# A tuned two-block network kernel on one core: elementwise tensor arithmetic taken off GpSimd and given to VectorE

## The chip, the core and the metric

The kernel runs on one NeuronCore of one Trainium2 chip. The core has five engines with an instruction queue each, which start their instructions in order: PE (TensorE, matrix products; PEld is its load of weights), DVE (VectorE), ACT (ScalarE), POOL (GpSimd) and SP (SyncE, which here only issues DMAs). The engines meet through semaphores. The metric is the device time of one execution in microseconds; lower is better.

## What is computed

A stream of 512 tokens by 1024 features goes through two blocks, all in float32. In outline:

```
first block, twice (l = 0, 1):
  h += rms_norm( mixer(rms_norm(h)) )         # dilated attention | short conv | gated delta rule, 4 heads
  h += rms_norm( cross_attention(rms_norm(h), rms_norm(mem)) )
  h += rms_norm( (silu(g) * u) @ w_down )     # g, u = split(rms_norm(h) @ w_gate_up), hidden width 2816
second block:
  x += gate * even_mixer(modulated rms_norm(x), ctx)   # two grouped attentions, rope, gates
  x += gate * odd_mixer(modulated rms_norm(x), ctx)    # 31-tap depthwise conv over tokens | 8 heads of local attention
  out = rms_norm(x)
```

Every `rms_norm` divides by the root of the mean square over the 1024 features plus 1e-6 and multiplies by a gain.

## The kernel before

The stream lies transposed: features on the 128 partitions, in 8 chunks, 512 tokens along the free axis (`hT`, 8 x 128 x 512). A matrix product keeps float32 accuracy in three passes: weights and inputs are each split in a high part and a low part of fewer bits (`wh` + `wl`, `xh` + `xl`), and `mm3` (L288 to L290) adds wh·xh, wh·xl and wl·xh in PSUM. `weight` loads a tile of 128 x 1024 weights (`wr`), ACT rounds it to `wh` (L258), DVE subtracts for `wl` (L262). So each of some 420 tiles of weights costs DVE one subtraction, and PE can't finish the tile's products before it is done.

The work of a chain (a softmax, a residual, a delta-rule step) is interleaved with independent products: `fill` holds generators, and `pump` takes a step of one between two steps of the chain. The kernel is recorded in that order; a scheduler then sets the order within each engine by when operands should be ready, so that the queues are not simply the order of the text. Which engine an elementwise operation runs on is written in the code: a number of tables (`SV`, `CSV`, `PSV`, `RPL`, `GV`, `CD`, `FIN`) say for single steps whether DVE or GpSimd does them.

The places that matter below:

- `residual`: for each of 8 chunks DVE makes `rt` = om · post · R (L397), then `hT += rt` (L398), on GpSimd for chunks 1, 3, 5, 7; ACT and DVE split the new chunk (L377, L378); PE multiplies it. `sumsq` squares a chunk on ACT and adds it to `acc`, mostly on GpSimd (L368); a product with ones sums over partitions (L355).
- `gdn_pair`: two heads of the gated delta rule. A chain of 30 short DVE instructions eliminates 16 columns (L982, L983), two more write `TT` (L985), PE transposes it (L993), GpSimd masks `AT` into `W` (L999). Meanwhile the fill projects the next heads: evacuation, convolution of 4 taps and `silu` (L440 to L444), whose last product is on GpSimd.
- `ffn`: per 128 hidden columns, DVE takes the gate product out of PSUM times R (`fg`, L427), `silu` follows, DVE takes the linear half out of PSUM times R (`fu`, L427), GpSimd multiplies the two (L1178). R is 1/rms of the norm before it.
- the odd mixer: 32 items of attention (softmax L707 to L725, transposes L735), and between them the 31 taps of `conv31` for 4 chunks. Chunks 0 to 2 use one fused DVE instruction per tap (L1715); chunk 3 multiplies on ACT (L1718) and adds on GpSimd (L1719). GpSimd also adds the column mask to the bias (L1642) and makes one of two low parts of each key (L695, beside DVE's L693).
- the end: `final` normalizes in two halves of 256 tokens, some pieces on GpSimd (L1218).

Of the kernel before, what the change touches and what calls it, by code (L numbers as in the profile page):

```python
# [29 lines left out]
SV = (2, 4, 6, 7)  # L30
CSV = (1, 3, 5, 7)
TS, TB = 2, 2
WP, XP = 1, 2
CD = 3
# [14 lines left out]
PSV = (1, 3, 5, 7)  # L49
LOH = 1  # L50
FIN = ((1, 0, 2), (1, 2, 4), (0, 4, 6), (0, 6, 8)), ((1, 0, 2), (1, 2, 4), (1, 4, 6), (0, 6, 7), (1, 7, 8))
Y1, Y2, Y3 = 2, 1, 2
GV = (1, 2, 3)
RPL = (1, 3, 5, 7)

# ------------------------------------------------------------------ small parameters, one column block each
# [14 lines left out]
def _consts():  # L71
    """Tables that depend on shapes alone."""
# [50 lines left out]
def _host(inp):  # L123
    """Lays the inputs out: transposes, tiles of the weights, rows and columns in the order of their use."""
# [22 lines left out]
    # second block  # L147
# [60 lines left out]
class Net:  # L208
    def __init__(self, ctx, tc, a, out):
# [21 lines left out]
        nc.vector.memset(self.epst[:, 2:3], EPS * 256.0)  # L231
        self.mod = [b.tile([128, 24, 2], F32, name=f"mod{i}") for i in range(2)]
# [15 lines left out]
    # ---- tiles of the weights, split in two parts of 12 bits  # L248
# [43 lines left out]
    def gemm_g(self, ap, x, done, n=512, k=KC, tag="g"):  # L292
        """done([128 columns of w]^T x, in PSUM), in pieces"""
# [22 lines left out]
    # ---- products that follow the chunks of their input as they are made  # L316
# [18 lines left out]
    # ---- work that is put between the steps of a chain  # L335
# [15 lines left out]
    # ---- 1/sqrt of (scale * sum over partitions + bias), on all partitions  # L351
    def rsqrt_of(self, ss, out, scale, epscol, n=512, lhs=None):
        nc = self.nc
        ps = self.bps()[:, :n]
        nc.tensor.matmul(ps, self.ones if lhs is None else lhs, ss, start=True, stop=True)  # L355
        nc.scalar.activation(out, ps, AF.Ln, bias=self.epst[:, epscol:epscol + 1], scale=scale)
        nc.scalar.activation(out, out, AF.Exp, scale=-0.5)

    def sumsq(self, acc, src, first, eng=None, t=None):
# [20 lines left out]
    # ---- residual: hT += norm(om) * post; the next norm's statistics in R and its input, without 1/rms, in xh + xl  # L380
    def residual_stat(self, c, ps, acc):
        nc = self.nc
        nc.scalar.copy(self.om[:, c], ps)
        self.sumsq(acc, ps, c == 0, nc.vector if c == KC - 1 else None)

    def residual(self, acc, post, pre=None, R=None, scale=1.0 / D, epscol=0, chunk=2):
# [3 lines left out]
        with self.hp(HA):  # L390
            self.rsqrt_of(acc, Rp, 1.0 / D, 0)
# [11 lines left out]
        if pre is not None:  # L403
            self.prestat(R, scale, epscol, PSV)

    def prestat(self, R, scale=1.0 / D, epscol=0, dve=()):
        nc = self.nc
        acc = self.tmp("acc2", bufs=1)
        for c in range(KC):
            self.sumsq(acc, self.hT[:, c], c == 0, nc.vector if c in dve else None)  # L410
        self.rsqrt_of(acc, R, scale, epscol)

    def start(self, tiles):
# [10 lines left out]
        self.prestat(self.R, dve=SV)  # L424
# [12 lines left out]
    def silu(self, out, x, t, mul=None):  # L437
        """out = x * sigmoid(x), x in SBUF"""
# [5 lines left out]
        (mul or nc.vector).tensor_mul(out, x, t)  # L444

    # ---- tables of the partial rotary embedding
# [30 lines left out]
    # ---- first block  # L477
    def first(self, dbg=None):
# [5 lines left out]
        for l in range(2):  # L484
# [5 lines left out]
            if l == 0:  # L490
                with tc.tile_pool(name="md", bufs=1) as p:
# [7 lines left out]
                    self.residual(acc, "f_post0", "mix_pre1", self.R, chunk=1)  # L499
                    self.drain()  # L500
                if dbg and dbg(self, f"h3_{l}"): return
            else:
# [6 lines left out]
                with tc.tile_pool(name="ctx", bufs=1) as p:  # L509
                    self.fill = [self.ctx_stream(p)]  # L510
                    acc = self.xo_ffn(l, dbg, 1)
                    self.residual(acc, "f_post1", chunk=1)
# [10 lines left out]
    def xo_ffn(self, l, dbg, chunk):  # L523
# [4 lines left out]
        self.residual(acc, f"x_post{l}", f"f_pre{l}", self.R, chunk=chunk)  # L528
# [44 lines left out]
    def mix_out(self, l):  # L573
        """the first half of the mixer's outputs as input of its last product"""
# [8 lines left out]
    def shortconv(self, l, c, w, x, p):  # L583
# [7 lines left out]
        nc.gpsimd.tensor_mul(cp[:, 2:514], t, u)  # L591
# [6 lines left out]
        nc.gpsimd.tensor_mul(self.om[:, 2 + c], o, b)  # L598

    def dilated_in(self, l, w, x, p):  # L600
# [3 lines left out]
        with self.tc.tile_pool(name=f"dx{l}", bufs=1) as q:  # L604
# [4 lines left out]
            def rotate(xs, g):  # L609
                for c in range(2):  # L610
                    d = qk[:, 2 * g + c]
                    nc.gpsimd.tensor_mul(xs[:, c], xs[:, c], CS[:, 1])
# [49 lines left out]
    def to_tok(self, v, out, n):  # L662
        """v [128 features, n*128 tokens] -> out [128 tokens, n, 128 features]"""
# [6 lines left out]
    def qstack(self, q, p, scale, n=512, bufs=2):  # L670
        """the two heads of a chunk: their high and low parts over 128 partitions"""
# [11 lines left out]
    def kstack(self, k, p, bufs=2, out=None, n=512, off=0):  # L683
# [4 lines left out]
        for e in range(2):  # L688
# [38 lines left out]
    def ptrans(self, P, out, idx):  # L727
        """128-key blocks of P [128 queries, keys] -> out [128 keys, block, 128 queries], block i to idx[i]"""
# [16 lines left out]
    # ---- gated delta rule, four heads  # L745
# [54 lines left out]
    def gdn_norm(self, l, O, i, p):  # L800
        """norm over the width of each head, times the gate, for 128 tokens"""
# [16 lines left out]
    def gdn_gate(self, l, h, w, x):  # L818
        o = self.om[:, 4 + h]
        yield from self.gemm_g(w[24 + h], x, lambda ps: self.evacR(o, ps))  # L820
        self.silu(o, o, self.tmp("rt"), self.nc.gpsimd)

    def gdn_rows(self, l, x, p, cols, rh, rl):
# [11 lines left out]
        # beta  # L835
# [3 lines left out]
        # -exp(a_log) * softplus(a + dt_bias)  # L839
# [12 lines left out]
        # exp(decay) and exp(decay at the chunk's end - decay)  # L852
# [4 lines left out]
        # cols: [token, pair, quantity, head]  # L857
# [4 lines left out]
        # beta * exp(decay)  # L862
# [8 lines left out]
    def gdn_in(self, l, h, w, x, p, f):  # L871
        """q, k, v of a head: projection, causal convolution, silu, norm of q and k"""
# [900 lines left out]
```

## Time and profile before

| | |
|---|---|
| time, median of 3 runs | 2667.45 us (2666.31 to 2668.95) |
| span of the profiled execution, first to last instruction | 2663.9 us, 3.5 us under the median |
| busy | PE 2493.7 (94%), DVE 1799.1 (68%), ACT 1374.8 (52%), POOL 562.6 (21%) |
| mean granted TensorE clock | 0.977 of full speed |

The profile does not give a device time for its own execution; the 3.5 us between its span and the median are taken as what lies around the span. Busy time counts a stretch once even if two instructions overlap. PE's busy time contains matmuls that wait in its pipeline, so 94% is no measure of how near it is to its peak.

### The profile page before, as it was taken

Reading aid. Unit: us, or ns where it says so; the run is one execution under the profiler, and the core shown is the slowest. Engines: PE = TensorE matmul, PEld = TensorE weight load, DVE = VectorE, ACT = ScalarE, POOL = GpSimd, SP = SyncE. Lnnn points to the kernel's source line nnn. Section 1 sums busy time; section 2 is a strip of 40 time slices with the busy share of each in tenths; the row PEclk is TensorE's granted clock in tenths of the full one; section 3 lists DMA queues with packets and bytes.
Section 4 is the critical chain, followed back from the end, with each engine's and each line's share of the span. In section 5 each row is a group of like instructions: output and inputs, shape, how many; then the busy total and the mean of one; then the engine's idle time right before and its main releaser. Section 6 shows DMA issues by size and latency. Waiting matters only on the chain. (4 is left out here: it accounts for less than half of the span.)

```text
span 2663.9 us, 35466 instructions
## 1 busy us (share of the span) xinstructions
PE 2493.7 (94%) x13052; PEld 2020.3 (76%) x13052; DVE 1799.1 (68%) x3064; ACT 1374.8 (52%) x2629; POOL 562.6 (21%) x437
## 2 busy tenths in 40 slices
PE   8999999899999999899998999999979999898898
PEld 6677788667888666777887778788867888686786
DVE  7985665389554578765756656665587666589964
ACT  6653554443433456434545544445356766447674
POOL 2343120120100323422102100002032012115432
PEclk9999999999999999999999999999989999899999
DMA  5132132456333433212412233234232012221111
GB/s 170 51 78 65 58 129 99 127 180 211 108 107 91 143 98 78 54 54 87 136 62 96 79 96 111 83 100 138 86 122 89 25 40 66 79 79 46 50 60 64
DMA packets 82781, 246.02 MB, mean 92 GB/s; under 512 B 13736, under 2 KB 25128, under 8 KB 81456
## 3 DMA queue, kind: packets, MB, share of 16 engines
q1 hardware_dynamic: 79344, 240.41, 28.8%
q0 software_dynamic: 704, 2.17, 0.5%
q10 hardware_dynamic: 2560, 1.18, 0.3%
q8 instruction: 103, 1.69, 0.3%
q14 instruction: 70, 0.57, 0.1%
HBM read 237.68 MB, written 2.89 MB: 90 GB/s over the span
## 5 line engine op out<-in xcount | busy, mean ns | idle before, releaser
L288 PE MATMUL g<-xh,wh 128*128 128x512 f32 (+1 forms) x1960 | 781.2, 400 | 28.7 <-ACT wh L258 9.0
L289 PE MATMUL g<-xl,wh 128*128 128x512 f32 (+1 forms) x1960 | 781.2, 399 | 8.5 <-DVE xl L378 4.8
L290 PE MATMUL g<-xh,wl 128*128 128x512 f32 (+1 forms) x1960 | 777.2, 397 | 0.0
L258 ACT CAST wh<-wr 128x1024 fp32r<-128x1024 f32 (+4 forms) x422 | 396.9, 944 | 551.5 <-PE g L289 415.8
L262 DVE TENSOR_TENSOR wl<-wr,wh 128x1024 fp32r<-128x1024 f32 (+4 forms) x422 | 494.5, 1175 | 178.8 <-ACT wh L258 176.7
L288 PEld LDWEIGHTS g<-xh,wh 128*128 128x128 f32 x1960 | 371.9, 190 | 116.1 <-ACT xh L377 9.0
L289 PEld LDWEIGHTS g<-xl,wh 128*128 128x128 f32 x1960 | 374.4, 191 | 89.7 <-DVE xl L378 9.2
L290 PEld LDWEIGHTS g<-xh,wl 128*128 128x128 f32 x1960 | 373.7, 191 | 79.2 <-issue 4.8
L1178 POOL TENSOR_TENSOR fu<-fu,fg 128x512 f32<-128x512 f32 x44 | 68.1, 1548 | 615.9 <-ACT wh L258 342.5
L368 POOL TENSOR_TENSOR acc<-acc,sq 128x512 f32<-128x512 f32 x68 | 102.6, 1509 | 403.6 <-ACT sq L367 378.5
L288 PE MATMUL g<-yh,wh 128*128 128x512 f32 x352 | 140.2, 399 | 6.8 <-DVE om L1161 2.7
L290 PE MATMUL g<-yh,wl 128*128 128x512 f32 x352 | 139.1, 396 | 2.1 <-DVE wl L262 2.1
L289 PE MATMUL g<-yl,wh 128*128 128x512 f32 x352 | 138.7, 395 | 0.0
L735 PE MATMUL b<-ident,P 128*128 128x128 f32 x608 | 93.8, 280 | 32.8 <-DVE P L725 15.1
L735 PEld LDWEIGHTS b<-ident,P 128*128 128x128 f32 x608 | 69.1, 142 | 61.4 <-issue 35.3
L741 ACT COPY pt<-b 128x512 f32<-128x512 f32 (+3 forms) x224 | 92.1, 451 | 43.9 <-PE b L735 42.8
L1161 DVE TENSOR_TENSOR om<-om,g 128x512 f32<-128x512 f32 x80 | 54.8, 685 | 64.1 <-PE g L290 63.6
L290 PE MATMUL s<-ch,wl 128*128 128x256 f32 x288 | 83.6, 290 | 10.2 <-DVE wl L262 10.2
L441 ACT ACTIVATE rt<-rt 128x512 f32<-128x512 f32 x76 | 48.1, 632 | 81.8 <-DVE rt L440 81.4
L719 ACT ACTIVATE P<-P,st 128x512 f32<-128x512 f32 (+4 forms) x96 | 66.1, 689 | 37.9 <-DVE st L713 24.4
L1382 PE MATMUL b<-pt,V 128*64 128x128 f32 x672 | 85.2, 275 | 0.0
L288 PE MATMUL s<-ch,wh 128*128 128x256 f32 x288 | 84.9, 295 | 0.0
(432 smaller groups left out, 4774.4 us busy)
## 6 DMA issues: line engine op xcount, KB each, us to landing
wr<-in_w_gu_dram SPq DMA_DIRECT2D x88, 512.0 KB, 3.3
wr<-in_w_in_dram SPq DMA_DIRECT2D x56, 512.0 KB, 3.3
wr<-in_ev_in_dram SPq DMA_DIRECT2D x40, 512.0 KB, 3.2
wr<-in_od_in_dram SPq DMA_DIRECT2D x36, 512.0 KB, 3.5
wr<-in_w_xkv_dram SPq DMA_DIRECT2D x32, 512.0 KB, 3.2
mw<-in_mod_w_dram SPq DMA_DIRECT2D x24, 512.0 KB, 3.5
mw<-in_mod_t_dram SPq DMA_DIRECT2D x24, 512.0 KB, 3.4
wr<-in_w_down_dram SPq DMA_DIRECT2D x56, 192.0 KB, 2.4
```

The lines of the kernel that those rows point to most:

```text
L258: nc.scalar.copy(hi[:, :k], raw[:, :k])
L262: nc.vector.tensor_sub(lo[:, c:e], raw[:, c:e], hi[:, c:e].bitcast(F32))
L288: mm(ps, wh, xh, start=first, stop=False)
L289: mm(ps, wh, xl, start=False, stop=False)
L290: mm(ps, wl, xh, start=False, stop=last)
L368: (eng or nc.gpsimd).tensor_add(acc, acc, t)
L719: nc.scalar.activation(P[:, c], src[i], AF.Exp, bias=one(2), accum_out=one(3 + i))
L735: nc.tensor.transpose(ps[:, 128 * i:128 * i + 128], P[:, 128 * (j + i):128 * (j + i) + 128], self.ident)
L741: nc.scalar.copy(out[:, idx[j + i]:idx[j + i] + e - i], ps[:, 128 * i:128 * e].rearrange("p (a b) -> p a b", b=128))
L1161: nc.vector.tensor_add(self.om[:, c], self.om[:, c], ps)
L1178: nc.gpsimd.tensor_mul(u, u, g)
L1382: nc.tensor.matmul(o[s], v, PT[e][:, k], start=j == 0, stop=j == len(blocks) - 1)
```

## The change

Every elementwise tensor instruction on GpSimd goes to DVE; only its memsets and DMAs stay. The tables that chose an engine vanish. Two places change their arithmetic. In `ffn` the linear half is no longer multiplied by R: DVE multiplies the PSUM tile by `fg` directly, and one multiplication per tile is gone. The output is then larger by 1/R per token, which the norm behind the feed-forward divides out, except for its epsilon; so the norm's sum of squares starts from epsilon over R squared (`zacc`, one ACT instruction from the sums that R itself comes from) and takes no other epsilon. In `conv31` chunk 3 uses the fused taps too.

```
     def sumsq(self, acc, src, first, t=None):
...
             nc.scalar.activation(t, src, AF.Square)
-            (eng or nc.gpsimd).tensor_add(acc, acc, t)
+            nc.vector.tensor_add(acc, acc, t)
...
                 nc.vector.scalar_tensor_tensor(t, self.om[:, c], self.sm(post, c), Rp, ALU.mult, ALU.mult)
-                (nc.gpsimd if c in RPL else nc.vector).tensor_add(self.hT[:, c], self.hT[:, c], t)
+                nc.vector.tensor_add(self.hT[:, c], self.hT[:, c], t)
...
+        ps = self.rsqrt_of(acc, R, scale, epscol)
+        if keep:
+            self.zacc = self.tmp("acc", bufs=1)
+            nc.scalar.activation(self.zacc, ps, AF.Identity, bias=self.epst[:, 3:4], scale=8.0 * EPS / D)
...
-        (mul or nc.vector).tensor_mul(out, x, t)
+        nc.vector.tensor_mul(out, x, t)
...
-            nc.gpsimd.tensor_sub(lo[o, c], k[s], h[s, c].bitcast(F32))
+            nc.vector.tensor_sub(lo[o, c], k[s], h[s, c].bitcast(F32))
...
-                nc.gpsimd.tensor_mul(P3(M[e]), P3(AT[:, e]), bc(lev[:, lvl]))
+                nc.vector.tensor_mul(P3(M[e]), P3(AT[:, e]), bc(lev[:, lvl]))
...
-                    self.evacR(u, self.gemm(a["w_gu"][l][2 * j + 1], x))
-                    nc.gpsimd.tensor_mul(u, u, g)
+                    nc.vector.tensor_mul(u, self.gemm(a["w_gu"][l][2 * j + 1], x), g)
...
-            if c < CD:
-                nc.vector.scalar_tensor_tensor(o[:, lo:hi], src, dw(k), o[:, lo:hi], ALU.mult, ALU.add)
-            else:
-                s = self.tmp("sq")[:, lo:hi]
-                nc.scalar.activation(s, src, AF.Copy, scale=dw(k))
-                nc.gpsimd.tensor_add(o[:, lo:hi], o[:, lo:hi], s)
+            nc.vector.scalar_tensor_tensor(o[:, lo:hi], src, dw(k), o[:, lo:hi], ALU.mult, ALU.add)
```

The same exchange of engine is made in `prestat`, `colstat`, `gate`, `rope2`, `shortconv`, `rotate`, the rest of `gdn_pair`, `mem_kv`, `conv_norm`, the bias of the odd mixer and `final`.

In numbers of instructions: GpSimd's queue goes from 442 to 61, DVE's from 3066 to 3406, ACT's from 2399 to 2370; PE's and SP's have as many as before. The scheduler sets the orders anew; three places on DVE's queue follow.

The end of the elimination of the first pair of heads in layer 0 (`c` and `pr` are the columns being eliminated, `wl` and `wr` weights, `W` the masked matrix, `TT` what PE transposes next). Before:

```order
L262 TENSOR_TENSOR wl_2012<-wr_2009,wh_2011 128x1024
L983 TENSOR_TENSOR c_164_1288<-c_164_1288,pr_1289 128x8x3
L982 TENSOR_TENSOR pr_1289<-W_1107,c_164_1288 128x8x2
L983 TENSOR_TENSOR c_164_1288<-c_164_1288,pr_1289 128x8x2
L982 TENSOR_TENSOR pr_1289<-W_1107,c_164_1288 128x8
L983 TENSOR_TENSOR c_164_1288<-c_164_1288,pr_1289 128x8
L985 TENSOR_TENSOR TT_1108<-c_164_1288,d_214 128x512 x2
L427 TENSOR_TENSOR om<-g_1777,R 128x512
```

And now:

```order
L984 TENSOR_TENSOR c_164_1289<-c_164_1289,pr_1290 128x8x2
L257 TENSOR_TENSOR wl_1860<-wr_1857,wh_1859 128x1024
L983 TENSOR_TENSOR pr_1290<-W_1108,c_164_1289 128x8
L257 TENSOR_TENSOR wl_1924<-wr_1921,wh_1923 128x1024
L984 TENSOR_TENSOR c_164_1289<-c_164_1289,pr_1290 128x8
L1000 TENSOR_TENSOR W_1108<-AT_1107,lev_213 128x512
L986 TENSOR_TENSOR TT_1109<-c_164_1289,d_215 128x512 x2
L1000 TENSOR_TENSOR W_1108<-AT_1107,lev_213 128x512
L445 TENSOR_TENSOR cvv_1640<-cvv_1640,rt_1645 128x512
```

The masks into `W` and the products of `silu` (L445) now stand in DVE's queue around `TT`.

The residual after the second feed-forward (`acc` with the number 17xx sums the squares for the next norm). Before:

```order
L397 SCALAR_TENSOR_TENSOR rt_16234<-om,small,R 128x512
L397 SCALAR_TENSOR_TENSOR rt_16250<-om,small,R 128x512
L398 TENSOR_TENSOR hT<-hT,rt_16234 128x512
L262 TENSOR_TENSOR wl_16302<-wr_16299,wh_16301 128x1024
L397 SCALAR_TENSOR_TENSOR rt_16253<-om,small,R 128x512
```

And now:

```order
L394 SCALAR_TENSOR_TENSOR rt_16197<-om,small,R 128x512
L394 SCALAR_TENSOR_TENSOR rt_16213<-om,small,R 128x512
L395 TENSOR_TENSOR hT<-hT,rt_16197 128x512
L395 TENSOR_TENSOR hT<-hT,rt_16213 128x512
L394 SCALAR_TENSOR_TENSOR rt_16216<-om,small,R 128x512
```

Both additions to `hT` of a pair of chunks are DVE's now, one behind the other.

The odd mixer, between two items of attention (`cu`, `ckv` and `R` hold the inputs of the conv's chunks, `K` the keys' low parts, `P` and `st` belong to the softmax). Before:

```order
L1715 SCALAR_TENSOR_TENSOR om<-ckv,small,om 128x510
L724 RECIPROCAL st_20321<-st_20321 128x1
L693 TENSOR_TENSOR K_2314_20204<-rt_20213,K_2313_20203 64x512
L725 TENSOR_SCALAR P_20320<-P_20320,st_20321 128x768
L713 TENSOR_SCALAR st_20396<-st_20396 128x1
L1715 SCALAR_TENSOR_TENSOR om<-ckv,small,om 128x511 x2
L1715 SCALAR_TENSOR_TENSOR om<-R,small,om 128x511
```

And now:

```order
L726 TENSOR_SCALAR P_20226<-P_20226,st_20227 128x768
L708 TENSOR_REDUCE st_20270<-s_20249 128x1
L694 TENSOR_TENSOR K_2310_20157<-rt_20168,K_2309_20156 64x512
L714 TENSOR_SCALAR st_20270<-st_20270 128x1
L696 TENSOR_TENSOR K_2310_20157<-rt_20168,K_2309_20156 64x512
L694 TENSOR_TENSOR K_2312_20159<-rt_20168,K_2311_20158 64x512
L696 TENSOR_TENSOR K_2312_20159<-rt_20168,K_2311_20158 64x512
```

Four low parts of keys stand there where DVE had two, and the taps of `cu` stand among those of the other chunks.

## Rows read from the trace of the kernel before

**Rows 1.** The page: busy time, share of the span, instructions of each engine.

```profile
PE 2493.7 (94%) x13052; PEld 2020.3 (76%) x13052; DVE 1799.1 (68%) x3064; ACT 1374.8 (52%) x2629; POOL 562.6 (21%) x437
```

**Rows 2.** Four stretches: us; busy (instructions) of PE, PEld, DVE, ACT, POOL; granted clock.

```profile
140.00:180.00 40.00, 33.81 (x146) 26.70 (x145) 38.65 (x71) 21.84 (x33) 13.02 (x13) 0.91 0.33 89
...
666.00:732.60 66.60, 66.60 (x294) 54.76 (x293) 39.34 (x49) 27.32 (x37) 9.84 (x6) 1.00 0.35 108
...
1928.00:1985.00 57.00, 38.79 (x211) 31.63 (x210) 50.03 (x61) 32.19 (x57) 21.38 (x13) 0.79 0.38 123
...
2399.00:2532.00 133.00, 111.33 (x648) 90.76 (x648) 131.12 (x225) 89.52 (x202) 68.42 (x46) 0.95 0.16 51
```

**Rows 3.** PE's waits: line, what it waited for, total us, times, longest.

```profile
PE b L993 <- DVE TT L985: 20.1, 6, 6.1
...
PE b L355 <- DVE acc L368: 12.5, 6, 3.6
...
PE s L290 <- DVE wl L262: 11.2, 3, 7.7
...
PE g L288 <- ACT xh L377: 6.8, 6, 2.9
```

**Rows 4.** Single lines: instructions, their ns min/median/max, first and last start.

```profile
L398 POOL TENSOR_TENSOR hT<-hT,rt x24: 1262/1680/2714, 353.6 to 1970.7; 128x512 f32<-128x512 f32 x24
L398 DVE TENSOR_TENSOR hT<-hT,rt x24: 674/682/1791, 354.9 to 1970.5; 128x512 f32<-128x512 f32 x24
```

**Rows 5.** Timeline, DVE and POOL, around 151 us: start, us, instruction.

```profile
150.96 1.37 DVE L982 TENSOR_TENSOR pr<-W,c 128x104 f32<-128x104 f32 x1
152.92 0.25 DVE L983 TENSOR_TENSOR c<-c,pr 128x104 f32<-128x104 f32 x1
...
150.89 1.32 POOL L444 TENSOR_TENSOR cvv<-cvv,rt 128x512 f32<-128x512 f32 x1 [2.38 <-ACT rt L443]
```

**Rows 6.** Timeline, DVE and POOL, at the end of that elimination.

```profile
173.30 3.32 DVE L985 TENSOR_TENSOR TT<-c,d 128x512 f32<-128x512 f32 x2
...
173.14 2.93 POOL L999 TENSOR_TENSOR W<-AT,lev 128x512 f32<-128x512 f32 x2 [1.98 <-DMA wr<-in_w_in_dram]
```

**Rows 7.** Groups on DVE and POOL, 2399 to 2532 us: count, busy us, mean ns.

```profile
L1715 DVE SCALAR_TENSOR_TENSOR om<-ckv,small,om 128x507 f32<-128x507 f32 (+14 forms) x41 | 37.2, 927 | 0.0
L725 DVE TENSOR_SCALAR P<-P,st 128x768 f32<-128x768 f32 x21 | 21.3, 1012 | 0.1
L1715 DVE SCALAR_TENSOR_TENSOR om<-R,small,om 128x511 f32<-128x511 f32 (+14 forms) x15 | 15.3, 1023 | 0.0
L262 DVE TENSOR_TENSOR wl<-wr,wh 128x1024 fp32r<-128x1024 f32 x11 | 15.2, 1380 | 0.0
...
L693 DVE TENSOR_TENSOR K<-rt,K 64x512 fp32r<-64x512 f32 x6 | 9.1, 1520 | 0.1
L723 DVE TENSOR_TENSOR st<-st 128x1 f32<-128x1 f32 x20 | 8.6, 432 | 0.1
...
L1719 POOL TENSOR_TENSOR om<-om,sq 128x500 f32<-128x500 f32 (+14 forms) x27 | 40.5, 1499 | 28.7 <-ACT sq L1718 28.0
L1642 POOL TENSOR_TENSOR rpb<-rpb,colm 128x896 f32<-128x896 f32 x4 | 9.1, 2264 | 2.2 <-DMA rpb<-in_rpb_dram 2.2
```

**Rows 8.** Timeline, DVE, with POOL idle from 2502.6 to 2505.1 us.

```profile
2502.65 1.20 DVE L262 TENSOR_TENSOR wl<-wr,wh 128x1024 fp32r<-128x1024 f32 x1
2503.77 0.61 DVE L725 TENSOR_SCALAR P<-P,st 128x768 f32<-128x768 f32 x1
2504.30 0.73 DVE L1715 SCALAR_TENSOR_TENSOR om<-R,small,om 128x499 f32<-128x499 f32 x1
2504.95 0.15 DVE L723 TENSOR_TENSOR st<-st 128x1 f32<-128x1 f32 x1
```

**Rows 9.** The page: the feed-forward's product on POOL; the last column is idle before.

```profile
L1178 POOL TENSOR_TENSOR fu<-fu,fg 128x512 f32<-128x512 f32 x44 | 68.1, 1548 | 615.9 <-ACT wh L258 342.5
```

**Rows 10.** Timeline, DVE, the last norm's second half.

```profile
2653.85 1.48 DVE L368 TENSOR_TENSOR acc<-acc,sq 128x256 f32<-128x256 f32 x1
```

More of the change, by code (lines that the diff above doesn't have):

```diff
@@ L355, in rsqrt_of, with sumsq @@
         nc.tensor.matmul(ps, self.ones if lhs is None else lhs, ss, start=True, stop=True)
-        nc.scalar.activation(out, ps, AF.Ln, bias=self.epst[:, epscol:epscol + 1], scale=scale)
+        bias = 0.0 if epscol is None else self.epst[:, epscol:epscol + 1]
+        nc.scalar.activation(out, ps, AF.Ln, bias=bias, scale=scale)
         nc.scalar.activation(out, out, AF.Exp, scale=-0.5)
-    def sumsq(self, acc, src, first, eng=None, t=None):
+        return ps
+    def sumsq(self, acc, src, first, t=None):
         nc = self.nc
@@ L383, in residual_stat, with residual @@
         nc.scalar.copy(self.om[:, c], ps)
-        self.sumsq(acc, ps, c == 0, nc.vector if c == KC - 1 else None)
-    def residual(self, acc, post, pre=None, R=None, scale=1.0 / D, epscol=0, chunk=2):
+        self.sumsq(acc, ps, c == 0)
+    def residual(self, acc, post, pre=None, R=None, scale=1.0 / D, epscol=0, chunk=2, aeps=0, keep=False):
         nc = self.nc
@@ L390, in residual @@
         with self.hp(HA):
-            self.rsqrt_of(acc, Rp, 1.0 / D, 0)
+            self.rsqrt_of(acc, Rp, 1.0 / D, aeps)
         self.pump(3)
@@ L435, in out_proj, with silu @@
         return acc
-    def silu(self, out, x, t, mul=None):
+    def silu(self, out, x, t):
         nc = self.nc
@@ L498, in first @@
                     self.begin([w[1][c] for c in range(TB)], XT[5])
-                    self.residual(acc, "f_post0", "mix_pre1", self.R, chunk=1)
+                    self.residual(acc, "f_post0", "mix_pre1", self.R, chunk=1, aeps=None)
                     self.drain()
@@ L511, in first @@
                     acc = self.xo_ffn(l, dbg, 1)
-                    self.residual(acc, "f_post1", chunk=1)
+                    self.residual(acc, "f_post1", chunk=1, aeps=None)
                     if dbg and dbg(self, f"h3_{l}"): return
@@ L527, in xo_ffn @@
         self.begin([w[c] for c in range(TB)], XT[1 + l])
-        self.residual(acc, f"x_post{l}", f"f_pre{l}", self.R, chunk=chunk)
+        self.residual(acc, f"x_post{l}", f"f_pre{l}", self.R, chunk=chunk, keep=True)
         if dbg: dbg(self, f"h2_{l}")
@@ L889, in gdn_in @@
             t = self.tmp("rt")
-            self.silu(o, o, t, nc.gpsimd)
+            self.silu(o, o, t)
             if n != "v":
@@ L1140, in ffn @@
         x = (self.xh, self.xl)
-        acc = self.tmp("acc", bufs=1)
+        acc = self.zacc
         n = 0
@@ L1162, in down @@
                     if hi == HC:
-                        self.sumsq(acc, self.om[:, c], c == 0, nc.vector if c == KC - 1 else None)
+                        self.sumsq(acc, self.om[:, c], False)
                 step()
@@ L1306, in colstat @@
         for c in range(KC):
-            self.sumsq(acc, src[:, c], c == 0, self.nc.vector if c in CSV else None)
+            self.sumsq(acc, src[:, c], c == 0)
         R = self.tmp("Rp", bufs=1)[:, :n] if R is None else R
@@ L1351, in gate @@
         t = self.tmp("sq")[:, :n]
-        self.silu(t, g, t, eng)
-        eng.tensor_mul(o, o, t)
+        self.silu(t, g, t)
+        nc.vector.tensor_mul(o, o, t)
     def attend(self, sp, Q, K, i, e, pieces):
@@ L1509, in gate @@
         def gate(m, j):
-            yield from self.gemm_g(a["ev_in"][10 * m + 6 + j], x, lambda ps: self.gate(ps, self.om[:, 4 * m + j], S, nc.vector if m and j in GV else None))
+            yield from self.gemm_g(a["ev_in"][10 * m + 6 + j], x, lambda ps: self.gate(ps, self.om[:, 4 * m + j], S))
         self.fill = [kv(0), q(0, 0)]
@@ L1619, in gate @@
         def gate(j):
-            yield from self.gemm_g(w[24 + j], x, lambda ps: self.gate(ps, self.om[:, 4 + j], S, nc.vector if j in GV else None))
+            yield from self.gemm_g(w[24 + j], x, lambda ps: self.gate(ps, self.om[:, 4 + j], S))
         self.fill = [qkv(0)]
@@ L1704, in conv31 @@
         yield
-        if c < CD:
-            nc.vector.tensor_scalar(o, u, dw(15), self.sm("dwb", c), ALU.mult, ALU.add)
-        else:
-            nc.scalar.activation(o, u, AF.Identity, bias=self.sm("dwb", c), scale=dw(15))
+        nc.vector.tensor_scalar(o, u, dw(15), self.sm("dwb", c), ALU.mult, ALU.add)
         for k in range(31):
@@ L1746, in conv_norm @@
             t = self.tmp("sq")
-            self.silu(o, o, t, nc.gpsimd)
+            self.silu(o, o, t)
             yield from self.gemm_g(w[8 + c], x, lambda ps: self.gate(ps, o, S))
```

63 lines of the change are left out of this document (27 added, 36 removed).

## The prediction

> **What bounds the kernel now.** I read the page first. PE is busy 2493.7 of the 2663.9 us [rows 1], so at most 170.2 us is idle on PE, and the change leaves PE's instructions as they are in number. DVE is busy 1799.1 us and POOL 562.6 us [rows 1]: over the whole span DVE has room, but that is a mean. So next I cut the span into stretches [rows 2]. There the reader is to see three kinds. In the feed-forward (666.0 to 732.6) PE is busy for all of the 66.6 us, at clock 1.00: nothing that DVE or POOL does there can shorten it. In the odd mixer (2399 to 2532) DVE is busy 131.12 of 133 us and PE 111.33: DVE is the bound. At the first pair of delta-rule heads (140 to 180) DVE is busy 38.65 of 40 us and PE 33.81; at 1928 to 1985 DVE has 50.03 of 57 and PE 38.79, at a granted clock of 0.79. So this kernel is bound by PE in most places and by DVE in a few, and those few decide. The third view is PE's list of waits [rows 3]: the change touches 20.1 us behind `TT`, 12.5 us behind `acc`, 11.2 us behind `wl` in the scores' products (one wait of 7.7), 6.8 us behind `xh` from ACT, which in `residual` comes after `hT += rt`.
>
> **What POOL costs DVE.** An instruction of 128x512 from two operands takes POOL 1.680 us in the median of the 24 of L398, and DVE 0.682 in the median for the other 24 of the same line, but DVE's reach up to 1.791 [rows 4]. The timeline shows why: L982 and L983 have the same small shape, and the one that starts 0.07 us behind a POOL instruction takes 1.37 us, ending near the POOL instruction's end, while the one that starts when POOL is idle takes 0.25 [rows 5]. The two writes of `TT`, 0.69 each when free, take 3.32 together beside two masks on POOL of 2.93 together [rows 6]. So a DVE instruction of this kind that overlaps a POOL instruction is held for most of it. The change takes DVE about 0.6 us per moved instruction and gives back what POOL's instructions held. Which is larger must be asked stretch by stretch, and it matters only where DVE sets the end.
>
> **Odd mixer, DVE-bound.** Refund: with POOL idle, a tap takes 0.73, L725 0.61, L723 0.15, `wl` 1.20 [rows 8]. Against the means of the stretch [rows 7]: taps 41 x (0.927 - 0.73) = 8.1 and 15 x (1.023 - 0.73) = 4.4; L725 21 x (1.012 - 0.61) = 8.4; L723 20 x (0.432 - 0.15) = 5.6; L693 6 x (1.520 - 0.68), with the 0.68 of a free 128x512 [rows 4], = 5.0; `wl` 11 x (1.380 - 1.20) = 2.0. Together 33.5; I add 3 for the groups not listed (an estimate by their share of DVE's time): 36.5. Charge: POOL did 46 instructions there [rows 2]. 27 are taps of chunk 3 [rows 7], which as fused taps I take at 0.65 each (free ones start that far apart: 2504.30 to 2504.95 [rows 8]), 17.6. Four bias additions of 128x896 [rows 7] at 0.60 x 896/512 = 1.05 are 4.2. The other 15 at 0.60 or less (two instructions of 128x512 in a row overlap by some 0.08) are 8.8. Together 30.6. Net -6. It is a difference of two large sums, so its bounds are wide: all of PE's idle time, -22 (133 less 111.33), and +30.6 if no refund comes. I take the sum, because rows 7 and 8 show both durations for the same lines. ACT loses the 27 products of chunk 3; it isn't the bound (89.52 of 133 [rows 2]).
>
> **Delta rule, -17.** PE waits 20.1 us for L985, six times, the longest 6.1 [rows 3], which is that of a first pair; I take the other layer's first pair as equal, so the other four are 8 us together. In the first pair POOL ran 13 instructions for 13.02 us inside a stretch that DVE fills [rows 2]. I give each first pair 4 of its 6 us (`TT` alone returns 3.32 - 1.3 = 2.0 [rows 6]; a chain instruction held as in [rows 5] returns 1.1, and some two or three of the 30 are; against that stand two masks and the products of `silu` that now stand in DVE's queue ahead of or around `TT`, 0.6 each). That is 8; half of the other four waits is 4. The masks of `W` and its scaling, which the chain runs through, become 0.6 in place of 1.3 to 1.5: 5 for eight pairs of instructions. Bounds: 0, if the elimination's 30 dependent steps set the time, and -25.
>
> **Residuals and norms, -8.** Of the 12.5 and 6.8 us behind `acc` and `xh` [rows 3], 1.0 of each 1.68 on POOL [rows 4] goes away: 12 waits at 0.7, about 8. Bounds 0 and -19.3. DVE's queue now holds two additions in a row for two chunks; that delays `xl` by 0.6, while `xh` comes 1.0 sooner.
>
> **1928 to 1985, -6.** POOL's 13 instructions there took 21.38 us [rows 2]; if each held DVE by 1.1 (as in [rows 5]) and costs it 0.6, DVE gains 13 x 0.5 = 6.5, and PE's wait of 7.7 for `wl` [rows 3] can take it. Bounds 0 and -7.7.
>
> **Feed-forward, 0.** Its product on POOL runs 44 times for 68.1 us, with POOL idle 615.9 us ahead of it [rows 9]; it vanishes and costs DVE nothing, since DVE's multiplication by R becomes the one by `fg`. DVE is busy 39.34 of 66.6 us there [rows 2], so that what DVE gets back is spare; without that cover the stage would have gained 44 x 0.7. `zacc` is one ACT instruction per layer off every chain but its own: the sum must wait for nothing else. **The end, -1:** the last addition to `acc` takes 1.48 beside POOL [rows 10], and 0.43 free (an estimate, 0.68 less the time of 256 columns).
>
> Sum: -6 - 17 - 8 - 6 - 1 = -38. These waits are not independent of others: after a wait goes, PE meets the next late operand, often ACT's, which the change leaves as it is. I take three quarters, a choice, -28.5. The profiled execution is 2663.9 + 3.5 = 2667.4 us, which is the median; so 2639.
>
> **Rivals.** (a) *Small gain, 2657.* DVE frees time, but the waits were set by more than DVE: only the parts where a moved instruction itself stood on the path shorten (residuals 8, end 1, and 1 for masks of `W`): -10. For it: PE's waits touched here are 50.6 us, so -38 asks for three quarters of them. Against it: the held instructions of [rows 5, 6] are in the chain itself. (b) *Larger gain, 2607.* PE runs at half clock where it has idled: clock 0.91 of 40 us, 0.79 of 57, 0.95 of 133 [rows 2] mean 7.2 + 23.9 + 13.3 = 44.4 us at the 1.2 GHz level, 22.2 us more than at 2.4. If the gaps close so far that the level stays at 2.4, this comes on top of all 38: -60. Against it: in each stretch most of the idle time would remain. (c) *Slower, 2712.* The long instructions of [rows 7] are long for another reason than POOL, and no refund comes. Then DVE, where it fills a stretch, pays: 30.6 in the odd mixer, 13 x 0.6 = 7.8 in each of two stretches like 140 to 180 and 7.8 at 1928, in all 54, less 9 that residuals and the end gain by POOL's own slowness: +45. It decides when less than about six tenths of the refund arrives (45 of 45 + 28.5). Against it: [rows 8] beside [rows 7], the same lines short with POOL idle. The Trainium skill (Perfetto Trace Analysis, Optimizing Scalar/DVE Operations) says that where DVE is saturated, handing some of its work to Scalar or even GpSimd may make sense; by that, taking it back in the odd mixer would cost the 30.6. The same paragraph warns that GpSimd and DVE share an SBUF read port, so that the exchange might not help; [rows 5] agree with the warning, 1.37 against 0.25. (d) *No change:* the refund falls short by half and the chains gain the rest, or the new order of the products puts a weight later and eats the gain.
>
> **Chances.** Forecast (-15 to -50) 0.61, (a) 0.17, (b) 0.06, (c) 0.09, (d) 0.07. A difference of 0.2% (5.3 us; 2662.1 and 2672.8) is about the least that a measurement of this kernel tells from none. Faster 0.61 + 0.17 + 0.06 = 0.84, same 0.07, slower 0.09. The range from 2610 to 2662 holds the forecast, (a) and the near part of (b); the forecast's own is 2617 to 2652.
>
> **What will show it.** Right: POOL busy under 20 us; DVE's total near 1800 to 1830, though it has some 340 instructions more; L985's pair in 1.3 us; L725 and taps in the odd mixer near 0.61 and 0.73, and the stage some 6 us shorter; waits for `TT` under 12 us; feed-forward stages as long as before. Wrong: the odd mixer longer with DVE still full, or DVE's mean per line unchanged with POOL silent; or the waits only renamed, to ACT or to the weights' DMA.

## The result, and the profile after

The changed kernel takes 2598.61 us (median of 4 runs, 2595.85 to 2603.0) against 2667.39 us before: 0.9743 of the time, 95% interval 0.973 to 0.9757, or 68.8 us less. The prediction said 2639 with a range of 2610 to 2662. The sign was right; the gain is 2.4 times the forecast one, and the time lies 11 us under the range.

The page of the changed kernel, busy time of each engine:

```profile
PE 2479.0 (95%) x13052; PEld 2011.0 (77%) x13052; DVE 1801.9 (69%) x3404; ACT 1350.9 (52%) x2600; POOL 21.7 (1%) x57
```

Against [rows 1], DVE does 340 instructions more in the same busy time (1799.1 before). So the holds that POOL laid on DVE cost as much as all the moved work. PE's idle time fell from 170.2 to 117.2 us, and its busy time by 14.7 us more for the same 13052 products, at a mean granted clock of 0.982 in place of 0.977.

Next, PE's waits of the changed kernel: line waited for, total us, times, longest.

```profile
PE g L285 <- DVE wl L257: 15.8, 8, 6.7
PE b L350 <- DVE acc L365: 11.7, 5, 3.4
...
PE s L285 <- DVE wl L257: 4.5, 3, 3.6
...
PE b L736 <- DVE st L714: 2.5, 3, 1.4
...
PE b L736 <- DVE P L726: 1.8, 2, 1.1
...
PE b L994 <- DVE TT L986: 0.8, 2, 0.5
```

The wait for `TT` that [rows 3] shows with 20.1 us is all but gone. So are, for the most part, two rows of the kernel before that [rows 3] did not show, PE's waits ahead of the transposes for the softmax's `P` and its maximum, here those of the odd mixer alone (2321.5 to 2547 us):

```profile
PE b L735 <- DVE st L713: 12.2, 6, 2.9
PE b L735 <- DVE P L725: 11.9, 8, 2.8
```

The changed kernel has in the same stretch:

```profile
PE g L285 <- DVE wl L257: 8.7, 3, 6.7
PE s L1360 <- ACT P L720: 3.3, 4, 1.6
```

So there a wait for a weight took the place of much of the wait for the softmax: a queue that is nearly full is late with something. The wait for `acc` hardly moved over the whole kernel (12.5 to 11.7).

Where the time went is best read from places that both traces have. PE's products with `ones` (or with `blk`) inside the norms stand in the same order in every kernel here; their starts cut the span into stretches with nearly the same work in each. The differences of the stretches' lengths from the changed kernel's, in us, worked out from these starts (a stretch is named by its end in the changed kernel and begins where the one above ends, the first at 142.4 us; `wide` is the run `ghost` below):

```
end     before  wide  u_gdn  u_norm  u_even  u_conv  only_ffn   what lies there
 185.5    8.1    7.7   10.0    0.2    -5.0    0.0      8.3      layer 0, first pair of heads
 339.3    2.4    7.3    0.7    4.4     8.4   -0.1      2.7      second pair, scan
 376.4    6.3    1.9    0.0    6.1     0.0    0.0      6.3      residual into cross attention
 890.8    5.6    0.1    1.0    1.8    -0.2   -0.7      1.4      cross attention, feed-forward 0
1016.0   -5.5    0.9   -4.2    2.2    -0.6    0.0     -5.5      residual, start of layer 1
1076.2   13.6    6.6   12.0    2.7     3.2    0.3     14.1      layer 1, first pair
1234.4    3.0    7.2    2.8   -4.6    -2.7   -0.1      3.3      second pair, scan
1271.5    6.3    1.9    0.0    6.3     0.0    0.0      6.3      residual into cross attention
1932.4    3.8   -0.1   -0.7    1.3    -0.9    0.5      2.2      cross attention, feed-forward 1, next norm
2050.5   -0.5    4.8    4.2    2.4    -1.4    3.1     -1.3      even mixer, begin
2265.0   13.5    4.4    0.0    0.1    12.1    0.0     12.7      even mixer, attention
2487.3    3.4   29.3    0.7   -0.1     6.6    1.3      2.9      odd mixer
2596.2    7.8    2.9    0.1    3.2     3.6    0.4      7.7      end
```

In the column of the kernel before, the delta rule, the two residuals and the even mixer's attention carry most of the gain; the odd mixer, which [rows 2] shows as DVE-bound, gives 3.4. Neighbouring stretches trade work where the order of products changed, so that single numbers of 3 or 4 us with opposite neighbours mean nothing. In the even mixer's attention the kernel before and `u_even` have 1348 products, the changed kernel 1337: some 1.7 us of these two numbers are moved products (an estimate, 11 times PE's mean of 0.157 us there). The begin of the even mixer is 3 to 4 us longer also in runs that change nothing there, such as `u_conv` (3.1, at a clock of 0.94 against 0.97), so a number of this size in that row says nothing either.

Some of these stretches in windows, first of the kernel before, then of the changed one (us; busy us and instructions of PE, PEld, DVE, ACT, POOL; granted clock, DMA share, GB/s):

```profile
350.10:393.50 43.40, 39.14 (x257) 35.29 (x256) 33.62 (x43) 23.71 (x38) 13.01 (x7) 0.96 0.34 113
...
2094.00:2321.50 227.50, 215.65 (x1348) 178.19 (x1347) 146.06 (x318) 140.67 (x327) 37.26 (x25) 0.98 0.19 59
```

```profile
339.70:376.80 37.10, 37.05 (x258) 33.98 (x257) 33.67 (x50) 23.66 (x38) 0.00 (x0) 1.00 0.40 131
1883.00:1933.40 50.40, 36.93 (x199) 29.64 (x198) 45.09 (x72) 30.09 (x52) 0.00 (x0) 0.77 0.41 132
2050.50:2265.00 214.50, 210.66 (x1338) 174.40 (x1339) 147.04 (x343) 141.58 (x329) 0.00 (x0) 1.00 0.19 59
2265.00:2487.30 222.30, 201.50 (x1073) 162.62 (x1073) 196.66 (x390) 120.45 (x259) 0.00 (x0) 0.95 0.20 65
```

In the residual (339.70) and the even mixer (2050.50) PE is now busy nearly all the time and its clock stays at 1.00. In the even mixer DVE had been busy 64% of the time, and the prediction did not look there.

### The profile page after: what moved, and what is told of

Read it like the earlier page. It is cut to its first block, busy times and chain, and to the rows that moved or that the text cites. A ratio compares the mean times of both kernels' runs of the same rounds, so it can differ in the third digit from the quotient of the medians.

```text
span 2596.2 us, 35112 instructions
## 1 busy us (share of the span) xinstructions
PE 2479.0 (95%) x13052; PEld 2011.0 (77%) x13052; DVE 1801.9 (69%) x3404; ACT 1350.9 (52%) x2600; POOL 21.7 (1%) x57
## 4 chain that ended last, share of the span: by engine, by line
PE 52%; DVE 6%; ACT 3%; issue 1%; DMA 1%; DVEq 0%; SPq 0%; ACTq 0%
PE g L285 11%; PE g L283 11%; PE g L284 11%; PE b L1381 4%; PE b L736 3%; PE s L283 2%; PE s L285 2%; PE s L284 2%; PE s L1360 1%; PE s L1361 1%; PE b L350 1%; DVE wl L257 1%; DVE om L1710 1%; DVE rt L394 0%; ACT wh L253 0%
## 5 line engine op out<-in xcount | busy, mean ns | idle before, releaser
L285 PE MATMUL g<-xh,wl 128*128 128x512 f32 (+1 forms) x1960 | 775.1, 396 | 15.1 <-DVE wl L257 15.1
L257 DVE TENSOR_TENSOR wl<-wr,wh 128x1024 fp32r<-128x1024 f32 (+4 forms) x422 | 458.7, 1090 | 165.2 <-ACT wh L253 162.8
L428 DVE TENSOR_TENSOR fg<-g,R 128x512 f32<-128x512 f32 x42 | 29.0, 691 | 93.5 <-PE g L285 93.0
L284 PE MATMUL s<-cl,wh 128*128 128x256 f32 x288 | 83.2, 289 | 0.0
L283 PEld LDWEIGHTS g<-yh,wh 128*128 128x128 f32 x352 | 66.7, 189 | 19.9 <-ACT ch L1291 5.2
```

Source lines behind the costliest of these rows:

```text
L257: nc.vector.tensor_sub(lo[:, c:e], raw[:, c:e], hi[:, c:e].bitcast(F32))
L283: mm(ps, wh, xh, start=first, stop=False)
L284: mm(ps, wh, xl, start=False, stop=False)
L285: mm(ps, wl, xh, start=False, stop=last)
L428: self.nc.vector.tensor_mul(out, ps, self.R[:, :ps.shape[-1]])
```

## Experiments

Times are medians; every batch had its own runs of the kernel before, with medians from 2665.89 to 2667.57. Intervals are of the ratio to that kernel.

**Idle additions (`ghost`).** In the changed kernel POOL got work that nobody waits for:

```
+    def ghost(self, x, y=None):
...
+        self.nc.gpsimd.tensor_add(t[:p, :n], x, x)
...
                 nc.vector.tensor_add(self.hT[:, c], self.hT[:, c], t)
+                if c in RPL:
+                    self.ghost(t)
```

> The changed kernel, and beside it, at the places where GpSimd had worked in the delta-rule pairs, in the products and residual behind the mixers, and in both mixers of the second block, one GpSimd addition that reads one of the same operands twice and writes into a scratch of its own that nobody reads. The result of the network is untouched; no chain runs through these additions. Theory H (GpSimd's instructions cost time by holding DVE's): at least half of the 68.8 us comes back, 2635 to 2700. Theory L (they cost time because they were slow links of chains): 2594 to 2604. Theory O (only the new order of the queues matters): 2594 to 2610, with DVE's durations per line as in the changed kernel.

Measured: 2673.32 us, ratio 1.0028 (1.0017 to 1.0038). The whole gain is gone. The page, and the DVE groups of its odd mixer (count, busy us, mean ns, idle before):

```profile
PE 2502.8 (94%) x13052; PEld 2020.3 (76%) x13052; DVE 1912.9 (72%) x3404; ACT 1351.3 (51%) x2600; POOL 276.4 (10%) x256
```

```profile
L1759 DVE SCALAR_TENSOR_TENSOR om<-ckv,small,om 128x507 f32<-128x507 f32 (+14 forms) x40 | 32.6, 846 | 0.0
...
L760 DVE TENSOR_SCALAR P<-P,st 128x768 f32<-128x768 f32 x16 | 13.6, 853 | 0.0
...
L758 DVE TENSOR_TENSOR st<-st 128x1 f32<-128x1 f32 x16 | 5.7, 353 | 2.9 <-ACT P L754 2.8
L727 DVE TENSOR_TENSOR K<-rt,K 64x512 fp32r<-64x512 f32 x4 | 5.3, 1320 | 0.5 <-ACT K L726 0.4
```

The same groups of the changed kernel without that work:

```profile
L1710 DVE SCALAR_TENSOR_TENSOR om<-ckv,small,om 128x507 f32<-128x507 f32 (+14 forms) x44 | 31.2, 737 | 0.0
...
L726 DVE TENSOR_SCALAR P<-P,st 128x768 f32<-128x768 f32 x21 | 12.9, 613 | 0.1
...
L694 DVE TENSOR_TENSOR K<-rt,K 64x512 fp32r<-64x512 f32 x6 | 4.1, 681 | 0.0
...
L724 DVE TENSOR_TENSOR st<-st 128x1 f32<-128x1 f32 x21 | 3.2, 155 | 4.0 <-ACT P L720 4.0
```

With 254.7 us more on POOL, DVE is 111.0 us longer busy on the same 3404 instructions. An instruction on one number per partition (`st`) that takes 0.155 us takes 0.353 in the mean. That is theory H. The rival that the idle additions kept buffers from being written again is small: ACT and DVE waited for them for 3.2 us in all.

**The same additions, 8 columns wide (`ghost8`).**

```
+            n, x = 8, x[:, :8]
```

> The run with GpSimd's idle-handed additions again, each at the same place and reading the same operand, but 8 columns wide. It has the same instructions, and so the same semaphores and nearly the same queues, without the long accesses. H: 2596 to 2612, and DVE's durations per line as in the changed kernel. If the new instructions' order or waits on buffers had made the loss of the wide ones (74.7 us over the changed kernel): above 2640.

Measured: 2603.73 us, ratio 0.9762 (0.9746 to 0.9778). By the two traces PE's 13052 products start in the same order in both runs, and 3398 of DVE's 3404 instructions do (by operation and operand, numbers left out). So 69.6 us between them is what the wide accesses do, and 5.1 us above the changed kernel is left for the order, the waits and the small instructions. Of these, 3.4 lie in the begin of the even mixer, where such a number says nothing. The page and one group of the odd mixer:

```profile
PE 2482.7 (95%) x13052; PEld 2013.2 (77%) x13052; DVE 1802.6 (69%) x3404; ACT 1350.5 (52%) x2600; POOL 109.7 (4%) x256
```

```profile
L1761 DVE SCALAR_TENSOR_TENSOR om<-ckv,small,om 128x507 f32<-128x507 f32 (+14 forms) x42 | 29.7, 737 | 0.0
```

POOL has as many instructions as in the wide run, and DVE isn't held by them.

**Short work on POOL (`short`).** The kernel before, with lines such as

```
-            (eng or nc.gpsimd).tensor_add(acc, acc, t)
+            e = acc.shape[-1] if eng else SHORT
+            (eng or nc.gpsimd).tensor_add(acc[:, :e], acc[:, :e], t[:, :e])
```

with `SHORT = 64`.

> The kernel before, with most of GpSimd's in-place arithmetic done on 64 columns alone (the other columns are left out, so the output differs): sums of squares, residual additions, the feed-forward's product, silu and gates outside the delta rule, rope, the bias, the conv's additions, the memory's norm. The engines and chains stay as before. H and L: POOL busy falls by more than half, and the time to 2590 to 2625. O: within 2655 to 2675, as the engines are those of before.

Measured: 2586.92 us, ratio 0.9702 (0.9688 to 0.9717), 3 us under what H and L gave. Each instruction runs on the engine that it had before, so the gain needs no change of engine. The queues do differ a little (12723 of PE's 13052 products stand at the same place as before), so that it takes `ghost` and `ghost8`, with PE's products in one order, to refute a gain from new queues alone (O). The chains' links on POOL are shorter here too: this run doesn't tell H from L. The odd mixer takes 27.7 us less here than in the changed kernel:

```profile
2276.80:2471.40 194.60, 189.76 (x1060) 156.09 (x1061) 169.94 (x333) 135.67 (x285) 39.36 (x52) 0.98 0.23 73
```

DVE has 169.94 us to do there against 196.66 in the changed kernel. Most of this is the charge of the moved work: in this stage it is real, and in the changed kernel it eats almost the whole refund.

**One part back at a time.** Each of these is the changed kernel with one group of instructions on POOL again, for example `u_conv`:

```
+            else:
+                s = self.tmp("sq")[:, lo:hi]
+                nc.scalar.activation(s, src, AF.Copy, scale=dw(k))
+                nc.gpsimd.tensor_add(o[:, lo:hi], o[:, lo:hi], s)
```

> The changed kernel, but chunk 3 of the conv multiplies on ACT and adds on GpSimd as before. H: GpSimd's 30 additions hold DVE in a stage that DVE fills, while DVE saves 30 taps: by the working of the prediction the two nearly cancel (30 x 0.65 = 19.5 saved, 30 x about 0.75 = 22 lost): 2596 to 2606. L: nothing waits for these additions and DVE saves 19.5 us: 2580 to 2596.

Measured: 2601.81 us (0.9757, 0.9742 to 0.9771), 3.2 over the changed kernel and inside what H said; L's 2580 to 2596 did not come. The 3.2 themselves are not clear of the noise (the intervals overlap), and in the odd mixer the run is 1.3 us longer.

```
-            nc.vector.tensor_mul(P3(Tw), P3(TT[:, e]), col(h, 2))
+            nc.gpsimd.tensor_mul(P3(Tw), P3(TT[:, e]), col(h, 2))
```

(and the masks, WQ, kd, the products of silu, of the short conv and of rotate.)

> The changed kernel with the work of the two mixers of the first block back on GpSimd (masks, WQ, kd and the scaled T of the delta rule, the last product of its silu, the short conv's products, rotate): 114 or so instructions. The stages around the delta rule gained about 8 + 2 us in the first layer and 16 in the second by the traces. H: 2620 to 2632. If other places hold this gain (order): under 2610.

Measured: 2626.65 us (0.985, 0.9836 to 0.9865), 28.0 over, as H said; 96 instructions came back, not 114.

```
-            nc.vector.tensor_add(acc, acc, t)
+            (eng or nc.gpsimd).tensor_add(acc, acc, t)
```

(and the residual additions, the memory's norm and the last norm's pieces, 113 instructions.)

> The changed kernel with residual additions, sums of squares, the memory's norm and the pieces of the last norm back on GpSimd. The two stretches from the norm behind the mixer to the next norm gained 6.3 us each (43.4 to 37.1), the end 7, the norms before and behind the feed-forwards some 2. H: 2615 to 2626; the forecast's own term of 8 + 1 would be 2607 to 2609.

Measured: 2621.05 us (0.9828, 0.9813 to 0.9843), 22.4 over, of which 6.1 and 6.3 in the two residuals ahead of cross attention.

```
-        self.silu(t, g, t)
-        nc.vector.tensor_mul(o, o, t)
+        self.silu(t, g, t, eng)
+        eng.tensor_mul(o, o, t)
```

(and rope, the bias, the keys' low parts, the sums of `conv_norm`, 99 instructions. Since `kstack` serves the first block too, some of these keys lie there.)

> The changed kernel with the second block's GpSimd work back, but for the conv's taps: gates, rope, bias plus column mask, half of the keys' low parts, the sums of conv_norm. The forecast had no term for the even mixer; the traces show 13 us gained there. H: 2610 to 2624 (13 in the even mixer, a few in the odd one). If the forecast was right to leave the even mixer out: under 2604.

Measured: 2616.39 us (0.981, 0.9796 to 0.9825), 17.8 over; 12.1 in the even mixer's attention, where the forecast had no term.

**The feed-forward alone (`only_ffn`).** The kernel before with

```
-                    self.evacR(u, self.gemm(a["w_gu"][l][2 * j + 1], x))
-                    nc.gpsimd.tensor_mul(u, u, g)
+                    nc.vector.tensor_mul(u, self.gemm(a["w_gu"][l][2 * j + 1], x), g)
```

> The kernel before with the feed-forward's change alone (no multiplication by R of the linear half, DVE multiplies out of PSUM, epsilon enters the next norm); all other GpSimd work as before. The prediction gave it 0, since PE fills the feed-forward: 2664 to 2668 by every theory. If the 4.1 us that the changed kernel gains between the norms around the first feed-forward belong to it: 2656 to 2662.

Measured: 2661.9 us (0.9985, 0.9976 to 0.9995), 4.7 less than before: a small gain, not 0. Its first 106 us of feed-forward 0, of the kernel before and then with this change:

```profile
560.00:666.00 106.00, 104.40 (x456) 84.96 (x455) 101.19 (x148) 41.89 (x59) 14.49 (x7) 1.00 0.65 203
```

```profile
560.00:666.00 106.00, 106.00 (x466) 87.31 (x465) 98.69 (x154) 45.22 (x65) 0.00 (x0) 1.00 0.71 220
```

The stretch in [rows 2] had been taken from the middle of the stage, where DVE has room. At its begin DVE is 95% busy with other interleaved work, and there PE did wait.

**Inside the residuals (`u_resid`)**: only `(nc.gpsimd if c in RPL else nc.vector).tensor_add(self.hT[:, c], self.hT[:, c], t)` back, 24 instructions.

> The changed kernel with the residual additions of chunks 1, 3, 5, 7 alone back on GpSimd (24 instructions). Theory C (in the residuals GpSimd was a slow link: ACT's queue stands behind it, then PE behind ACT): the two stretches of 37 us become 42 to 43 and the total 2606 to 2614; the run with idle additions showed 1.9 us in each of them. Rival (the sums of squares on GpSimd were the link, or holds of DVE): the two stretches stay under 39.5, total under 2605.

Measured: 2604.72 us (0.9765, 0.9751 to 0.978). The two stretches are 3.5 and 3.4 us longer, 40.5 us each, between the two expectations, and the total is just inside the rival's; the sums of squares must give most of the other 2.6 to 2.9 of the group. ACT's waits in the first stretch of the kernel before say how it comes about:

```profile
ACT xh L377 <- POOL hT L398: 6.3, 3, 2.5
...
ACT sq L367 <- POOL acc L368: 2.6, 2, 1.6
```

and PE's there:

```profile
PE b L1133 <- ACT vT L1129: 3.0, 1, 3.0
PE g L288 <- ACT xh L377: 0.8, 1, 0.8
PE g L289 <- DVE xl L378: 0.4, 1, 0.4
```

ACT's queue stands behind POOL, the copy of `vT` for the cross attention's values stands behind that, and PE waits for `vT`. These waits are 4.2 of the 6.3 us that the change took off the stretch; the other 2.1 are PE's busy time (39.14 to 37.05 for the same products), at a clock of 1.00 in place of 0.96. The wide idle additions cost only 1.9 us per stretch here, so this part is, by these rows, mostly a slow link, as theory C had it, and only in part a hold.

**Inside the even mixer.** The gates alone (`u_gate`, 36 instructions), rope and the keys' low parts (`u_krope`, 46), the bias (`u_bias`, 8):

```
-                    nc.vector.tensor_add(b3, b3, colm[:, None, :].to_broadcast([128, 14, 64]))
+                    nc.gpsimd.tensor_add(b3, b3, colm[:, None, :].to_broadcast([128, 14, 64]))
```

> The changed kernel with the gates of the second block alone back on GpSimd (10 to 18 instructions). The even mixer's second stretch was 12.1 us longer with gates, rope, bias and keys' low parts together back. If the gates hold DVE's softmax there: 4 or more of the 12 in that stretch, 2603 to 2610. If the low parts of the keys or the rope set it: under 2602.

> The changed kernel with rope's products and half of the keys' low parts alone back on GpSimd. Of the 12.1 us by which the second stretch of the even mixer was longer with the whole group back, the gates gave 4.2. If GpSimd's instructions hold DVE's softmax wherever they lie, each kind gives its share by its time on GpSimd (10.4 of 37 us): 2 to 4 us there, total 2601 to 2608. If the keys or rope are a slow link before the scores: 6 or more there.

> The changed kernel with the addition of the column mask to the bias (8 instructions of 128x896, 2.4 us each) alone back on GpSimd; three or four of them lie at the end of the even mixer. By the share of time on GpSimd (7.4 of 37 us): 2 to 3 us in that stretch, and 1 to 2 in the odd mixer: 2600 to 2606. If the queue's order made the difference: within 2 us of the changed kernel in both stretches.

Measured: 2606.26 (0.9767, 0.9751 to 0.9784), 2601.85 (0.976, 0.9744 to 0.9777) and 2607.15 us (0.9775, 0.9759 to 0.9791). The attention's stretch of the even mixer is longer by 4.2, 4.8 and 6.1 us, 15.1 together against 12.1 for all at once. Of the 4.8, again some 1.7 are moved products (1348 against 1337), which leaves 3.1. So the gates are as expected, and rope with the keys' low parts is within the 2 to 4 that sharing by time on POOL gave, under the 6 of a slow link. No kind is the link; each that runs on POOL there costs. The bias costs 6.1 where 2 to 3 was said, for three additions of 2.3 us. In its trace nothing waits for them, but DVE's subtractions for the keys' low parts do not get past them (start, us, instruction):

```profile
2209.18 0.42 DVE L700 TENSOR_TENSOR K<-dkc,K 64x256 fp32r<-64x256 f32 x1
...
2210.21 2.25 DVE L702 TENSOR_TENSOR K<-dkc,K 64x256 fp32r<-64x256 f32 x1
2212.48 2.25 DVE L700 TENSOR_TENSOR K<-dkc,K 64x256 fp32r<-64x256 f32 x1
2214.74 2.25 DVE L702 TENSOR_TENSOR K<-dkc,K 64x256 fp32r<-64x256 f32 x1
...
2209.86 6.85 POOL L1647 TENSOR_TENSOR rpb<-rpb,colm 128x896 f32<-128x896 f32 x3 [1086.23 <-PE g L290]
```

Each of the three takes 2.25 us in place of 0.42, one to each addition on POOL, so DVE's queue is 5.5 us late. PE is idle for 3.1 us more in the stretch and busy for 3.0 us more, at a clock of 0.98 against 1.00. So what a hold costs goes here by what stands in DVE's queue at that moment, and not by POOL's time alone.

**DVE or not DVE.** `act_scale` moves one step of the odd mixer's softmax from DVE to ACT, `act_all` that of all softmaxes:

```
-        nc.vector.tensor_scalar_mul(P, P, one(5))
+        nc.scalar.activation(P, P, AF.Copy, scale=one(5))
```

> The changed kernel, and the last step of the softmax in the odd mixer (P times 1/sum, 32 instructions of 128x768, 0.61 us each) on ACT instead of DVE. If DVE still sets the end of the odd mixer (in the run with short GpSimd work the stage was 27.7 us shorter with some 30 us less on DVE): 32 x 0.61 = 19.5 us less on DVE, stage 8 to 18 us shorter, 2580 to 2592. If PE or the chain of softmax sets it: 2595 to 2605, since ACT takes at least as long for the step.

> The same move in all softmaxes. In the even mixer and the dilated attention PE is near its bound and ACT is the busier of the two elementwise engines there (141 of 214 us against DVE's 147): no further gain, 0 to 5 us over the run that moves the odd mixer's alone.

Measured: 2589.21 us (0.9707, 0.9692 to 0.9721) and 2584.63 us (0.969, 0.9675 to 0.9704). The first total is as expected for a full DVE, but the odd mixer is only 6.6 us shorter, not 8 to 18:

```profile
2265.00:2480.70 215.70, 201.09 (x1072) 162.64 (x1072) 183.80 (x365) 138.27 (x280) 0.00 (x0) 0.94 0.21 67
```

DVE's 196.66 us fell by 12.9, the stage by half of that: DVE sets the end of the odd mixer for part of its length. The expectation for `act_all`, no further gain, failed: it is 4.6 us faster again (the two intervals just overlap), 14 us under the changed kernel and 83 under the kernel before, the fastest version here that computes everything.

## Why the prediction missed

**The mechanism was right** but for the two residuals, where POOL was above all a slow link. POOL's instructions hold DVE's, and taking them away returns to DVE about what the moved work costs it: DVE's busy time stays (forecast 1800 to 1830, measured 1801.9). The two idle-addition runs show the hold itself, 69.6 us between wide and narrow. L985's pair became 1.28 us (forecast 1.3); taps and L725 became 0.737 and 0.613 (forecast 0.73 and 0.61). Two of its signs failed: POOL is busy for 21.7 us, not under 20, and the feed-forward did get shorter. The Trainium skill (SBUF — State Buffer, Who interferes with whom) says that a DVE instruction with two SBUF inputs contends with a GpSimd instruction that reads SBUF, and that the loser blocks for the whole instruction; the means above (681 to 1320 ns for `K`) agree. The pair of L985, L986 in the changed kernel:

```profile
168.84 1.28 DVE L986 TENSOR_TENSOR TT<-c,d 128x512 f32<-128x512 f32 x2
```

**The sizes failed, all but two on the low side.** The sum of -38 was 31 us short before any discount. Its largest lacks are the norms (22.4 us against 9), the even mixer (13.5 against no term) and the delta rule (28.0 against 17). It also priced only PE's idle time, which fell by 53.0 us; that PE's busy time would fall too, by 14.7 us, stood in rival (b) alone.

- *"I take three quarters"* of -38. This discount was a choice without a row behind it. Undoing the parts one by one costs 28.0 + 22.4 + 17.8 + 3.2 us, and the feed-forward alone brings 4.7: 76.1 for a gain of 68.8. So the parts overlap one another by about a tenth. Without the discount the forecast would have been 2629, still 31 us too long.
- *Even mixer, no term.* It gave 13.5 us, some 1.7 of them moved products; taken whole, it would have put the low end at 2596.5, under the result. The stretch was left out because DVE was not full there and PE had no long wait. But PE was idle for 11.85 of its 227.5 us, in many short gaps, is idle for 3.84 of 214.5 now, and its busy time fell by 5.0 too. Runs with single kinds back show that no one of them is the cause; `u_bias` shows how a hold there reaches PE.
- *Delta rule, -17.* Measured 28.0 by undoing. I counted two thirds of the first pairs' waits and half of the others; of the 20.1 us [rows 3], 19.3 went. The masks that now stand in DVE's queue around `TT` cost nothing that shows.
- *Residuals, -8 and the end, -1.* By undoing 22.4 for all norms. I priced PE's waits for `acc`, which stayed (12.5 to 11.7), and for `xh`, and left out its waits for `vT` (5.9 us in the two residuals ahead of cross attention, now gone). The cause was in ACT's queue, one step further back, and the gain 12.6 us in these two stretches.
- *1928 to 1985, -6.* Failed the other way. PE's wait for `wl` of 7.7 us became one of 3.6 and others grew; the two stretches from 1883.0 to 1932.4 together are 1.2 us longer than before. DVE is as full there as it was (45.09 of 50.40 us), since it gave back no more than it took on. In `short`, where POOL's work is narrow and stays on POOL, these stretches take 42.9 us, with DVE busy for 35.95 of them.
- *Feed-forward, 0.* It gave 4.7; the row came from the stage's middle, and at its begin PE did wait for DVE.
- *Odd mixer, -6.* Right in size: 3.4 in the stretch. There refund and charge nearly cancel; `u_conv` and `short` (-27.7 in the stage) show both sides. By the page of the Trainium skill that the prediction weighed (Perfetto Trace Analysis, Optimizing Scalar/DVE Operations), handing DVE's work to GpSimd may pay where DVE is saturated, and may not because of the shared port: here the 30 taps bring no gain on GpSimd (3.2 us longer, not clear of the noise).

**The rivals.** (b) was nearest, 2607 against 2598.6, and its own step came in part: time at the 1.2 GHz level was 2 x (1 - 0.977) x 2663.9 = 122 us before and is 2 x (1 - 0.982) x 2596.2 = 93 us now (120 and 96 by the trace's clock to four places, 0.9775 and 0.9815), which is worth some 12 us, most of the 14.7 that PE's busy time fell by. But its stretches at 1928 and in the odd mixer kept their clocks (0.79 to 0.77, 0.95 to 0.95); it rose where no idle time is left, in the residuals and the even mixer. (c) is refuted by the idle additions, and by DVE's busy time, which did not grow: all of the refund came. (a) and (d) asked for 10 us or none, and are out by the size of the gain.

What stays open: how much of the 5 us between the changed kernel and the run with narrow additions is order and how much the additions themselves, and which instructions are held in the single gaps of the even mixer other than those that `u_bias` shows.

## What to carry to other kernels

Instructions on an engine that is 21% busy can cost a third engine's time, here PE's, by holding a second one's: look at the spread of durations of one line (0.25 and 1.37 us for the same shape), and test it by adding work that nobody waits for, wide and narrow. Price the return stretch by stretch, and in stretches where no engine is full too, since there it is the chain that is held. Where a wait vanishes, follow it back over in-order queues: PE's wait for ACT was ACT's wait for GpSimd.

## Not expected of the hardware

A GpSimd instruction of 8 columns takes 0.20 to 0.58 us on its own engine, by the means of its groups, and leaves DVE's durations as they are (0.737 for a tap); one of 512 columns that reads a single tile, 1.2 to 1.4 us long, holds even DVE instructions with one tensor operand (L726: 0.613 to 0.853 us in the mean).
